# A hybrid diffusion step on one core: plain products for the feed-forward output weights, in groups of 4, 4 and 3 tile pairs

## The chip, the cores and the metric

One core of a Trainium2 chip runs the whole program in one launch. The metric is the device time of one execution in microseconds (us), the median of several. The engines named below are PE (matrix products), PEld (PE's weight loads), DVE (the vector engine), ACT (the scalar engine), POOL (GpSimd) and SP, whose queue issues the loads of the weights.

## The reference, cut to what matters

Two layers, each a mixer and then a SwiGLU feed-forward part. 512 latent and 128 context tokens go through the same weights, so a product has 640 token columns, kept as two halves of 320. The model width is 1024 (8 tiles of 128), the hidden width 2816 (22 tiles).

```python
def swiglu(h, w_in, w_out):
    gate, up = jnp.split(h @ w_in, 2, axis=-1)
    return (jax.nn.silu(gate) * up) @ w_out
...
        h = rms_norm(x, norm_ffn[l]) * (1.0 + sc2) + sh2
        x = x + g2 * swiglu(h, w_ffn_in[l], w_ffn_out[l])
```

## The kernel before, in words

Everything is float32. A float32 product is made of three products of rounded numbers: each weight tile and each activation tile is cut into a high part (`hi`, an ACT cast, L284 for weights and L450 for activations) and a low part (`lo`, what the cast left, a DVE subtraction, L285 and L451), and PE adds hi·hi, hi·lo and lo·hi. A matmul is 128x128 weights by 320 columns.

**Input side.** Hidden tile f needs its gate and its up weights, 2 x 8 tiles. For f = 0 they are taken plainly (96 matmuls). For the other 21 tiles, called blocks here (key `fs`), the two weight matrices, halved in width, and the two token halves form a 2x2 by 2x2 block product, which is done with seven products in place of eight (`quads` and `chained`): 7 x 4 x 3 = 84 matmuls where plain ones take 96. In return the weights are cut in seven pieces, four of which are sums or differences made first (`st`, L307: one by DVE, three by POOL), and the seven results are put together through three PSUM banks (ACT copies at L623, DVE adds at L579, DVE and POOL products at L625 and L621). The activations' sums (`T` tiles) are made once for a layer.

**Output side.** Hidden tiles f and f+1 make a pair. Pairs are collected in groups, given by `FFG`. Once a group is complete, all eight output tiles add this group's share to the residual X (`resid`, L539). In the first three groups (of three pairs, key `ft`) this is again done with seven products for two output tiles: 7 x 3 x 3 = 63 matmuls in place of 72. The pair's activations then need four sums or differences (POOL, L566, tiles `tt`), and seven tiles are cut into hi and lo (`hf`). The last group (two pairs, key `fo`) is plain: both activation tiles are cut whole, the weights of an output tile are cut in one piece, and `lin` (L366) runs all its matmuls (six for each hidden tile, so 24 here) into a pair of PSUM banks while the other pair is read out; the final tile goes through `prod` (L347).

**Order of the work.** Weights come in one list (`plan`) and pass through three raw buffers (`wr`, `WR`=3), of which a block or an `ft` step takes two at once. Prepared pieces go to a ring of six slots (`wp`); `feed` prepares the next piece as soon as a slot is counted free. A scheduler orders each engine's instructions when the program is built; on the chip each engine runs its own list in that order, and SP issues its loads in order, each waiting until its raw buffer has been read. After each group the first block of the next one is computed before the group's output, so that PE has work while the last pair is cut.

Of the kernel before, what the change touches and what calls it, by code (L numbers as in the profile page):

```python
# [7 lines left out]
F32 = mybir.dt.float32  # L8
F32R = mybir.dt.float32r
# [18 lines left out]
WR = 3  # L28
# [2 lines left out]
POOLED = [("even", u) for u in (18, 19, 20, 21)]  # L31
GRB = 3
WA = 2
FFG = [3, 3, 3, 2]
FPLAIN = 1
ST = 4
TT = 3
FIRST = (4, 2, 2)

ORDER = {k: ("a11", "s1", "s2", "a12", "s3", "s4", "a22") for k in ("fs", "ft")}  # L40

CONST_COLS = {}
PARAM_COLS = {}
# [169 lines left out]
class K:  # L213
    def __init__(s, nc, tc, I, O, es, dbg=None):
        s.nc, s.tc, s.I, s.O, s.es = nc, tc, I, O, es
        s.dbg = dbg or {}
        s.n = 0
        s.flip, s.sp, s.turn, s.gate = False, None, 0, None
        s.base = s.pool("base", 1)
        s.w = s.pool("w", 1)  # L220
        s.pa = s.pool("pa", 1, space=PSUM).tile([P, 512], F32, name="pa")
        s.pe = es.enter_context(ExitStack())
        s.banks(3)
        s.plan, s.parts, s.gen = [], [], None
# [70 lines left out]
    def quads(s, key, src):  # L295

        nc = s.nc
        n = src[0].shape[1] // 2
        raw = [s.t(s.w, [P, 2 * n, P], "wr", WR) for _ in range(2)]
        for r, x in zip(raw, src):  # L300
            nc.sync.dma_start(r, x)
        a11, a12, a21, a22 = (r[:, i::2, :] if key[0] == "ft" else r[:, n * i:n * i + n, :] for r in raw for i in range(2))
        whole = {"a11": a11, "a12": a12, "a22": a22}

        def made(f, x, y, op, eng):
            whole[f] = s.t(s.sp, [P, 4, P], "st", ST)[:, :n]
            eng.tensor_tensor(whole[f], x, y, op=op)  # L307
        for f in ORDER[key[0]]:
            yield 1
            if f == "s1":  # L310
                made("s1", a21, a22, ALU.add, nc.vector)
                made("s2", whole["s1"], a11, ALU.subtract, nc.gpsimd)
            elif f == "s3":
                made("s3", a11, a21, ALU.subtract, nc.gpsimd)
# [255 lines left out]
    def ffn(s, l, X, norm, ef, nxt=None):  # L570
        nc = s.nc
        n2 = lambda a: a.rearrange("p (n c) -> p n c", n=2)
        with ExitStack() as es:
# [6 lines left out]

            def val(f):
                if f not in vs:
                    vs[f] = s.t(ap, [P, T], "a", 2)
                return vs[f]

            def evac(i, n, ps):
# [3 lines left out]
                else:  # L590
                    nc.vector.tensor_tensor(a, ps, a, op=ALU.mult)

            def up(f, plain):

                i = len(slots)
                w = s.t(norm.pool if i == 2 else ap, [P, 7, 2, 320], f"hf{i}", 1, F32R)
                slots.append(w)
                b11, b12, b21, b22 = (vs[f + k][:, 320 * j:320 * j + 320] for k in range(2) for j in range(2))
                vs.pop(f), vs.pop(f + 1)
                if not plain:  # L600
                    s.sevens(lambda: s.t(late[0], [P, 320], "tt", TT), lambda x: (w[:, HF[x], 0], w[:, HF[x], 1]), b11, b12, b21, b22)
                for x, nm in ((b11, "B11"), (b12, "B12"), (b21, "B21"), (b22, "B22")):
                    if plain or nm != "B12":
                        s.split(x, w[:, HF[nm], 0], w[:, HF[nm], 1])

            def block(f):

# [16 lines left out]
                          gate0, lambda ps: add(nc.vector, p5, ps, p5), gate1,  # L624
                          lambda ps: nc.vector.tensor_tensor(a0, ps, a0, op=ALU.mult))  # L625

            def out(key, o):

                def to(*parts):
                    def read(ps):  # L630
                        for c, n in parts:
                            s.resid(X[:, o + c, :], ps, g2, o + c, n)
                    return read
                s.chained(key, lambda b, k, p: slots[k][:, HF[b], p], len(slots),
                          to((0, 0)), to((1, 1)), to((0, 1)), to((0, 0)), to((1, 1)), to((0, 1)), to((1, 0)))

            def into(f):
                if f == 0:
                    s.together([("fi", l, 0, 0), ("fi", l, 0, 1), ("fi", l, 1, 0)][:FPLAIN + 1], norm.op, KD, evac,
# [13 lines left out]
            for kind, x in ffn_order():  # L653
                if kind == "in":
                    into(x)
                elif kind == "up":
                    up(x, False)
                elif kind == "upl":
                    up(x, True)
                elif kind == "out":  # L660
                    for o in range(0, KD, 2):
                        out(("ft", l, x, o), o)
                    slots.clear()
                else:
                    s.sp = None
                    ef.close()
                    if nxt:
                        res = nxt()
                    op = lambda k, n, p: slots[k // 2][:, HF[f"B{k % 2 + 1}{n + 1}"], p]
                    s.tail([("fo", l, x, o) for o in range(KD)], op, 2 * FFG[-1], X, g2, res)  # L670
        return res


HF = {n: i % 7 for i, n in enumerate(("B11", "B21", "B22", "T1", "T2", "T3", "T4", None, None, None, "B12"))}


def ffn_order():

    r, f, done = [], 0, set()

    def into(f):
        if f not in done:
            r.append(("in", f))
            done.add(f)
    for i, n in enumerate(FFG):
        last = i == len(FFG) - 1
        f0 = f
        for _ in range(n):
            into(f)
            into(f + 1)  # L690
            r.append(("upl" if last else "up", f))
            f += 2
        if not last:
            into(f)
        r.append(("last" if last else "out", f0))
    return r
# [77 lines left out]
class NormF(Norm):  # L774
# [2 lines left out]

    def init(s, pool):
        s.F = {n: s.k.t(pool, [P, 2, 4, 320], n, 1, F32R) for n in ("B11", "B21", "B22", "T1", "T2", "T3", "T4")}
        s.pool = pool  # L780
        w = s.k.t(pool, [P, 7, 2, 320], "hf2", 1, F32R).bitcast(F32)
        s.b0 = w[:, :4].rearrange("p k i t -> p (k i) t")
        s.free = [w[:, i // 2, i % 2] for i in range(8, 14)]

# [4 lines left out]
    def put(s, n):  # L789
        if n:  # L790
            s.spread(1)
        k, nc = s.k, s.k.nc

        def full(o, b_):
            t = s.scaled(o, n)
            for i, a, b in HALF[n]:
                r = slice(a - 320 * n, b - 320 * n)
                nc.scalar.activation(b_[:, r], t[:, r], AF.Identity, bias=s.sh[:, o, i:i + 1])

        if n == 0:  # L800
# [5 lines left out]
        w = [k.t(s.ap, [P, 7, 2, 320], f"hf{i}", 1, F32R) for i in range(2)]  # L806
# [8 lines left out]
        free = s.free + [w[0][:, i // 2, i % 2].bitcast(F32) for i in range(8, 14)]  # L815
# [11 lines left out]
def plan(I):  # L827
    r = []
# [7 lines left out]
    for l in range(2):  # L836
# [4 lines left out]
        for kind, x in ffn_order():  # L841
            if kind == "in":
                w = [I[f"w_fi{l}"][x, i] for i in range(2)]
                r += [(("fs", l, x), w, None)] if x >= FPLAIN else [(("fi", l, x, i), w[i], [P, KD, P]) for i in range(2)]
            elif kind == "out":
                n = 2 * FFG[0] if x == 0 else 2 * next(g for g, e in zip(FFG, np.cumsum(FFG)) if 2 * (e - g) == x)
                r += [(("ft", l, x, o), [I[f"w_fo{l}"][o + i, :, x:x + n, :] for i in range(2)], None) for o in range(0, KD, 2)]
            elif kind == "last":
                r += [(("fo", l, x, o), I[f"w_fo{l}"][o, :, x:, :], [P, NF - x, P]) for o in range(KD)]
    return r  # L850


# [1285 lines left out]
```

## Time and profile before

| what | us |
|---|---|
| three runs, median (lowest to highest) | 1908.77 (1907.92 to 1910.2) |
| the profiled execution | 1906.5 |
| its span, first to last instruction | 1904.6 |
| feed-forward part of layer 0, first to last matmul | about 633.4 to 1091.8 |
| feed-forward part of layer 1 | about 1434 to 1898.2 |

The span is what the trace shows; the execution's own time is 1.9 us longer, and the median of the three runs is 2.3 us above the profiled execution. Times in the trace count from the start of the span.

### The profile page before, as it was taken

The page shows a single profiled execution, that of the slowest core. Times are in us where ns is not written, and L with a number is a line of the kernel's source. Part 1 is how long each engine was busy: PE and PEld are TensorE (multiplying, and loading weights), DVE is VectorE, ACT ScalarE, POOL GpSimd, SP SyncE. Part 2 cuts the span into 40 slices and gives each one's busy share as a digit, 9 for nine tenths or more (in the row PEclk, how much of TensorE's full clock was granted, in tenths as well). Part 3 has the DMA queues.
Part 4 walks back from the last instruction along what each step waited for, and adds up shares of the span by engine and source line. Part 5 has one row for each costly group of instructions (what it writes and reads, how often), then busy time and mean ns, then how long its engine had stood idle before and what let it go on. Part 6 is the DMA issues. An engine that isn't in the chain of part 4 may idle for free.

```text
span 1904.6 us, 34515 instructions
## 1 busy us (share of the span) xinstructions
PE 1748.6 (92%) x13535; PEld 1586.8 (83%) x13535; DVE 1445.2 (76%) x2651; ACT 801.3 (42%) x1654; POOL 700.5 (37%) x586
## 2 busy tenths in 40 slices
PE   6999778889999899999999999799998899999999
PEld 4887667656669789988989989788997899899899
DVE  5579998656664898998988774744749988898885
ACT  3453126423363645454553442321426544444442
POOL 2034573210110555464563103322205654645540
PEclk9998888889999999999999999899998999999999
DMA  9564443796533022222222434221321222222222
GB/s 364 166 210 158 155 148 113 189 277 186 164 100 111 23 78 73 86 74 81 79 74 82 129 109 139 85 81 43 105 74 34 67 71 86 72 84 78 73 89 94
DMA packets 101638, 214.44 MB, mean 113 GB/s; under 512 B 8317, under 2 KB 44861, under 8 KB 100069
## 3 DMA queue, kind: packets, MB, share of 16 engines
q1 hardware_dynamic: 96852, 206.14, 35.1%
q10 hardware_dynamic: 4624, 6.11, 1.1%
q8 instruction: 106, 1.74, 0.4%
q14 instruction: 56, 0.45, 0.1%
HBM read 190.68 MB, written 21.54 MB: 111 GB/s over the span
## 4 chain that ended last, share of the span: by engine, by line
PE 38%; DVE 34%; DMA 14%; issue 6%; POOL 5%; ACT 3%; SPq 0%; DVEq 0%; ACTq 0%; POOLq 0%
PE mm L366 16%; DVE wp L285 14%; DVE hf L451 5%; DMA wr<-in_w_fi 5%; PE p L347 3%; DMA wr<-in_w_fo 3%; DVE x L539 3%; PE mm L347 3%; DMA wr<-in_w_ada 3%; PE pa L495 2%; PE p L1746 2%; DVE T L451 1%; DVE a L579 1%; PE p L1769 1%; DMA D<-grd 1%
## 5 line engine op out<-in xcount | busy, mean ns | idle before, releaser
L366 PE MATMUL mm<-hi,wp 128*128 128x320 f32 x1696 | 337.9, 317 | 1.1 <-DVE x L539 0.7
L285 DVE TENSOR_TENSOR wp<-wr,wp 128x512 fp32r<-128x512 f32 (+3 forms) x282 | 287.1, 1020 | 65.5 <-ACT wp L284 62.0
L284 ACT CAST wp<-wr 128x512 fp32r<-128x512 f32 (+2 forms) x286 | 198.9, 697 | 319.9 <-PE mm L366 186.5
L366 PEld LDWEIGHTS mm<-hi,wp 128*128 128x128 f32 x1696 | 273.2, 193 | 14.5 <-issue 9.8
L285 DVE TENSOR_TENSOR wp<-st,wp 128x512 fp32r<-128x512 f32 (+1 forms) x264 | 223.9, 861 | 1.1 <-ACT wp L284 0.3
L347 PE MATMUL p<-T,wp 128*128 128x320 f32 x1260 | 207.4, 312 | 17.4 <-ACT u L623 7.8
L347 PEld LDWEIGHTS p<-T,wp 128*128 128x128 f32 x1260 | 189.6, 189 | 24.2 <-ACT u L623 9.3
L366 PE MATMUL mm<-lo,wp 128*128 128x320 f32 x848 | 200.1, 316 | 0.2 <-DVE lo L451 0.2
L284 ACT CAST wp<-st 128x512 fp32r<-128x512 f32 (+1 forms) x264 | 147.5, 579 | 111.1 <-PE p L347 45.3
L307 POOL TENSOR_TENSOR st<-st,wr 128x512 f32<-128x512 f32 (+1 forms) x66 | 93.2, 1413 | 230.4 <-DVE st L307 203.3
L347 PE MATMUL p<-B,wp 128*128 128x320 f32 x888 | 152.2, 312 | 6.3 <-DVE wp L285 5.8
L347 PE MATMUL p<-hf,wp 128*128 128x320 f32 x954 | 155.0, 310 | 3.2 <-DVE wp L285 2.2
L347 PEld LDWEIGHTS p<-hf,wp 128*128 128x128 f32 x954 | 142.8, 188 | 7.1 <-DVE wp L285 4.9
L366 PEld LDWEIGHTS mm<-lo,wp 128*128 128x128 f32 x848 | 145.6, 192 | 1.5 <-DVE lo L451 0.5
L347 PEld LDWEIGHTS p<-B,wp 128*128 128x128 f32 x888 | 134.6, 188 | 11.1 <-DVE wp L285 9.7
L347 PE MATMUL mm<-T,wp 128*128 128x320 f32 x756 | 125.5, 315 | 8.9 <-ACT u L623 2.9
L347 PEld LDWEIGHTS mm<-T,wp 128*128 128x128 f32 x756 | 114.9, 191 | 12.8 <-DVE p L579 4.7
L539 DVE SCALAR_TENSOR_TENSOR x<-mm,ada,x 128x128 f32<-128x128 f32 (+2 forms) x194 | 73.4, 419 | 61.6 <-PE mm L366 57.6
L347 PE MATMUL mm<-B,wp 128*128 128x320 f32 x624 | 106.1, 314 | 9.9 <-DVE a L625 7.5
L347 PE MATMUL mm<-hf,wp 128*128 128x320 f32 x630 | 106.8, 311 | 4.7 <-DVE x L539 2.5
L347 PEld LDWEIGHTS mm<-B,wp 128*128 128x128 f32 x624 | 96.3, 192 | 11.6 <-DVE a L625 8.3
L621 POOL TENSOR_TENSOR a<-a,p 128x320 f32<-128x320 f32 x42 | 50.5, 1203 | 149.9 <-DVE p L579 80.1
(491 smaller groups left out, 3378.7 us busy)
## 6 DMA issues: line engine op xcount, KB each, us to landing
wr<-in_w_fi SPq DMA_DIRECT2D x88, 512.0 KB, 3.5
wa<-in_w_ada SPq DMA_DIRECT2D x52, 512.0 KB, 6.5
wr<-in_w_ada SPq DMA_DIRECT2D x44, 512.0 KB, 6.5
wr<-in_w_fo SPq DMA_DIRECT2D x48, 384.0 KB, 3.1
wr<-in_w_odd SPq DMA_DIRECT2D x25, 512.0 KB, 3.6
wr<-in_w_even SPq DMA_DIRECT2D x22, 512.0 KB, 4.8
J<-scr SPq DMA_DIRECT2D x20, 512.0 KB, 7.9
scr<-vk SPq DMA_DIRECT2D x8, 640.0 KB, 3.9
```

The source lines that it names most:

```text
L284: s.nc.scalar.copy(hi, raw)
L285: (eng or s.nc.vector).tensor_tensor(lo, raw, hi.bitcast(F32), op=ALU.subtract)
L307: eng.tensor_tensor(whole[f], x, y, op=op)
L347: s.nc.tensor.matmul(out, a[:, k, :], op(k, n, p), start=(k == 0 and q == 0 and not onto), stop=(k == nk - 1 and q == 2), skip_group_check ...
L366: s.nc.tensor.matmul(ps[:, n, :320], a[:, k, :], op(k, n, p), start=(k == 0 and q == 0), stop=(k == nk - 1 and q == 2))
L451: b = (eng or s.nc.vector).tensor_tensor(lo, full, hi.bitcast(F32), op=ALU.subtract)
L495: nc.tensor.matmul(ps[32 * g:32 * g + 32, :256], s.cs[:, k, :], w[:, g * 256:(g + 1) * 256], start=(k == 0), stop=(k == KD - 1))
L539: s.nc.vector.scalar_tensor_tensor(x[:, a:b], in0=ps[:, a - 320 * n:b - 320 * n], scalar=gate[:, k, i:i + 1], in1=x[:, a:b], op0=ALU.mult, ...
L579: add = lambda eng, o, x, y: eng.tensor_tensor(o, x, y, op=ALU.add)
L621: nc.gpsimd.tensor_tensor(a1, a1, p5, op=ALU.mult)
L1746: nc.tensor.matmul(sa, qT[:, a, t, :], kf[:, a, :512], start=True, stop=True)
L1769: nc.tensor.matmul(u[64 * a:64 * a + 64, 2, :], vt[:, j, (2 * b + a) * 64:(2 * b + a) * 64 + 64], pTs[a][:, j, :], start=(j == 4), stop=(j ...
```

## The change

Three things are edited. The output weights of all groups now take the plain path, and the groups are of 4, 4 and 3 pairs; so `out`, the seven products with key `ft`, and the four sums of each pair's activations are gone, a pair's two tiles are each cut whole (128 x 2 x 320), and a third buffer `a` holds the activations. The raw weights of the blocks go through a fourth buffer, `w2`, which lives in the feed-forward part's own memory: every fourth raw load of a block takes it. The temporary tiles of the `T` sums move to the space of the fourth pair.

```diff
-FFG = [3, 3, 3, 2]
+FFG = [4, 4, 3]
...
-        raw = [s.t(s.w, [P, 2 * n, P], "wr", WR) for _ in range(2)]
-        for r, x in zip(raw, src):
-            nc.sync.dma_start(r, x)
...
+        raw = []
+        for x in src:
+
+            s.raws = (s.raws + 1) % (WR + 1)
+            raw.append(s.t(s.w, [P, 2 * n, P], "wr", WR) if s.raws else s.t(s.sp, [P, 2 * n, P], "w2", 1))
+            nc.sync.dma_start(raw[-1], x)
...
-                    vs[f] = s.t(ap, [P, T], "a", 2)
+                    vs[f] = s.t(ap, [P, T], "a", 3)
...
-                if not plain:
-                    s.sevens(lambda: s.t(late[0], [P, 320], "tt", TT), lambda x: (w[:, HF[x], 0], w[:, HF[x], 1]), b11, b12, b21, b22)
-                for x, nm in ((b11, "B11"), (b12, "B12"), (b21, "B21"), (b22, "B22")):
-                    if plain or nm != "B12":
-                        s.split(x, w[:, HF[nm], 0], w[:, HF[nm], 1])
+                for k in range(2):
+                    x = n2(vs.pop(f + k))
+                    s.split(x, w[:, 2 * k:2 * k + 2, 0], w[:, 2 * k:2 * k + 2, 1])
...
-                elif kind == "out":
-                    for o in range(0, KD, 2):
-                        out(("ft", l, x, o), o)
...
+                    nk = 2 * len(slots)
+                    hid = list(slots)
+                    op = lambda k, n, p: hid[k // 2][:, 2 * (k % 2) + n, p]
                     slots.clear()
...
+                    keys = [("fo", l, x, o) for o in range(KD)]
+                    if kind == "out":
+                        s.tail(keys, op, nk, X, g2)
```

SP's list in layer 0's second group: the loads of three blocks before (two rows for a block; `wr` is the ring of three, the number only names the tile).

```order
L301 DMA wr_8414<-in_w_fi 128x1024
L301 DMA wr_8415<-in_w_fi 128x1024
L301 DMA wr_8571<-in_w_fi 128x1024
L301 DMA wr_8572<-in_w_fi 128x1024
L301 DMA wr_8705<-in_w_fi 128x1024
L301 DMA wr_8706<-in_w_fi 128x1024
```

The same place now.

```order
L304 DMA wr_8932<-in_w_fi 128x1024
L304 DMA w_8934<-in_w_fi 128x1024
L304 DMA wr_9071<-in_w_fi 128x1024
L304 DMA wr_9073<-in_w_fi 128x1024
L304 DMA wr_9205<-in_w_fi 128x1024
L304 DMA w_9207<-in_w_fi 128x1024
```

Every fourth load goes to the fourth buffer (`w`, the tile `w2`), so that the two loads of a block and the two of the next one never share a buffer.

DVE's list for one block of layer 0's second group before (`wp` a weight cut, `st` a sum of weights, `hf` a cut of activations, `tt` a difference of activations, `a`, `p` and `u` the block's results).

```order
L307 TENSOR_TENSOR st_8604<-wr_8572 128x512
L625 TENSOR_TENSOR a_8386<-p_8390,a_8386 128x320
L285 TENSOR_TENSOR wp_8568<-wr_8415,wp_8568 128x512
L285 TENSOR_TENSOR wp_8588<-wr_8571,wp_8588 128x512
L451 TENSOR_TENSOR hf_8520<-a_8386,hf_8520 128x320
L285 TENSOR_TENSOR wp_8608<-st_8604,wp_8608 128x512
L285 TENSOR_TENSOR wp_8625<-st_8606,wp_8625 128x512
L579 TENSOR_TENSOR a_8543<-p_8549,p_8544 128x320
L451 TENSOR_TENSOR hf_8520<-tt_8529,hf_8520 128x320
L451 TENSOR_TENSOR hf_8520<-tt_8533,hf_8520 128x320
L579 TENSOR_TENSOR a_8543<-mm_8548,u_8546 128x320
L285 TENSOR_TENSOR wp_8641<-wr_8571,wp_8641 128x512
```

And for a block at the same place now.

```order
L624 TENSOR_TENSOR a_8770<-mm_8774,a_8770 128x320
L285 TENSOR_TENSOR wp_8949<-wr_8932,wp_8949 128x512
L454 TENSOR_TENSOR hf_9038<-a_8770,hf_9038 128x2x320
L285 TENSOR_TENSOR wp_8969<-st_8965,wp_8969 128x512
L582 TENSOR_TENSOR a_8904<-p_8909,u_8907 128x320
L310 TENSOR_TENSOR st_9104<-wr_9073 128x512
L285 TENSOR_TENSOR wp_8986<-st_8967,wp_8986 128x512
L582 TENSOR_TENSOR a_8904<-mm_8910,p_8905 128x320
L285 TENSOR_TENSOR wp_9002<-wr_8932,wp_9002 128x512
L582 TENSOR_TENSOR p_8906<-mm_8908,p_8906 128x320
L285 TENSOR_TENSOR wp_9022<-st_9020,wp_9022 128x512
L285 TENSOR_TENSOR wp_9052<-st_9050,wp_9052 128x512
```

The cuts of `tt` are gone, and a tile of activations is cut whole. Before, the sum `st_8604` is cut five rows behind it; now `st_9104` is made a block ahead, and none of the rows shown uses it.

ACT's list around the cast of a pair's activations before (`u` is the copy that lets PE go on in the same bank).

```order
L623 COPY p_8679<-mm_8682 128x320
L284 CAST wp_8722<-wr_8705 128x512
L450 CAST hf_8811<-a_8543 128x320
L623 COPY u_8680<-p_8681 128x320
L284 CAST wp_8742<-st_8738 128x512
L284 CAST wp_8759<-st_8740 128x512
```

And now.

```order
L622 COPY p_9045<-p_9048 128x320
L284 CAST wp_9088<-wr_9071 128x512
L453 CAST hf_9038<-a_8904 128x2x320
L622 COPY u_9046<-p_9047 128x320
L284 CAST wp_9108<-st_9104 128x512
L284 CAST wp_9125<-st_9106 128x512
```

The order is the same: the copy `u` stands behind the cast `hf`, which is now twice as wide.

## Rows read from the trace of the kernel before

**Rows 1.** The page: engines' busy time, share of the span, instructions.

```profile
PE 1748.6 (92%) x13535; PEld 1586.8 (83%) x13535; DVE 1445.2 (76%) x2651; ACT 801.3 (42%) x1654; POOL 700.5 (37%) x586
```

**Rows 2.** Timeline, PE, layer 0's mixer output: start, length, instructions.

```profile
596.29 0.75 PE L366 MATMUL mm<-hi,wp 128*128 128x320 f32 x4
...
597.17 0.75 PE L366 MATMUL mm<-hi,wp 128*128 128x320 f32 x4
```

**Rows 3.** Windows, layer 0, matmuls on prepared weights: length, busy, count, clock.

```profile
633.40:690.00 56.60, 46.63 (x266) 0.91 0.13 38
...
859.00:907.00 48.00, 44.66 (x289) 1.00 0.27 73
```

**Rows 4.** The same windows for layer 1.

```profile
1434.00:1492.00 58.00, 46.89 (x266) 0.91 0.12 37
...
1592.00:1675.00 83.00, 75.54 (x486) 0.98 0.23 72
1675.00:1715.00 40.00, 39.89 (x273) 1.00 0.30 89
```

**Rows 5.** Windows, all engines, three input stretches.

```profile
core 0: us, PE busy (x) PEld busy (x) DVE busy (x) ACT busy (x) POOL busy (x), PEclk, DMA share, GB/s
784.40:859.00 74.60, 70.30 (x470) 68.59 (x468) 67.33 (x88) 37.97 (x82) 42.22 (x30) 1.00 0.27 82
...
1027.00:1066.00 39.00, 38.26 (x259) 37.74 (x258) 33.69 (x49) 19.66 (x41) 15.52 (x11) 1.00 0.27 81
1836.00:1868.00 32.00, 31.57 (x211) 30.98 (x212) 26.04 (x37) 16.70 (x36) 12.05 (x8) 1.00 0.26 78
```

**Rows 6.** Chain that ended last, 907 to 980.5 us, share by line.

```profile
by line: DVE wp L285 30.9%; DVE hf L451 17.4%; DMA wr<-in_w_fi 14.1%; issue 7.5%; PE p L347 6.4%; PE mm L347 5.0%; DVE a L579 4.9%; POOL a L621 3.5%; POOL tt L566 2.9%; DVE a L625 2.3%; ACT wp L284 1.4%; DVE st L307 1.2%; ACT hf L450 0.6%; 
```

**Rows 7.** Waits of the weight loads, 784.4 to 906 us: total, times, longest.

```profile
PEld p L347 <- DVE wp L285: 2.3, 4, 0.8
PEld p L347 <- DVE p L579: 2.2, 2, 1.8
```

**Rows 8.** Waits of DVE, the same stretch.

```profile
DVE st L307 <- DMA wr<-in_w_fi: 7.0, 5, 2.1
```

**Rows 9.** Groups by shape, the same stretch: busy us, mean ns.

```profile
L285 DVE TENSOR_TENSOR wp<-st,wp 128x512 fp32r<-128x512 f32 x24 | 24.5, 1041 | 0.1
...
L285 DVE TENSOR_TENSOR wp<-wr,wp 128x512 fp32r<-128x512 f32 x18 | 19.8, 1104 | 0.0
...
L451 DVE TENSOR_TENSOR hf<-a,hf 128x320 fp32r<-128x320 f32 x9 | 10.6, 1177 | 1.3 <-ACT hf L450 1.3
...
L451 DVE TENSOR_TENSOR hf<-tt,hf 128x320 fp32r<-128x320 f32 x12 | 8.6, 731 | 0.4 <-ACT hf L450 0.4
...
L307 DVE TENSOR_TENSOR st<-wr 128x512 f32<-128x512 f32 x6 | 4.2, 693 | 7.1 <-DMA wr<-in_w_fi 7.0
...
L579 DVE TENSOR_TENSOR p<-p,p 128x320 f32<-128x320 f32 x4 | 1.9, 480 | 0.0
```

**Rows 10.** Groups by shape, DVE, 1066 to 1092 us, where POOL rests.

```profile
L285 DVE TENSOR_TENSOR wp<-wr,wp 128x512 fp32r<-128x512 f32 x7 | 4.8, 682 | 1.3 <-PE mm L347 1.3
```

**Rows 11.** Groups by shape, DVE, 1389 to 1417 us, layer 1's mixer output.

```profile
L285 DVE TENSOR_TENSOR wp<-wr,wp 128x1024 fp32r<-128x1024 f32 x5 | 6.0, 1215 | 0.0
...
L539 DVE SCALAR_TENSOR_TENSOR x<-mm,ada,x 128x320 f32<-128x320 f32 x4 | 2.2, 549 | 11.3 <-PE mm L366 11.3
...
L539 DVE SCALAR_TENSOR_TENSOR x<-mm,ada,x 128x192 f32<-128x192 f32 x4 | 1.6, 408 | 0.0
```

**Rows 12.** Chain that ended last, the same stretch: start, us, what.

```profile
1389.40 28.39 PE mm L366 x192
```

**Rows 13.** Timeline at 959 us: ACT's queue and the matmul behind it.

```profile
959.27 0.46 ACT L450 CAST hf<-a 128x320 fp32r<-128x320 f32 x1 [3.48 <-DVE a L625]
959.64 0.42 ACT L623 COPY u<-mm 128x320 f32<-128x320 f32 x1
...
960.11 0.41 PE L347 MATMUL mm<-T,wp 128*128 128x320 f32 x1 [1.50 <-ACT u L623]
```

More of the change, by code (lines that the diff above doesn't have):

```diff
@@ L38 @@
 FIRST = (4, 2, 2)
-ORDER = {k: ("a11", "s1", "s2", "a12", "s3", "s4", "a22") for k in ("fs", "ft")}
+ORDER = {"fs": ("a11", "s1", "s2", "a12", "s3", "s4", "a22")}
 CONST_COLS = {}
@@ L217, in __init__ @@
         s.n = 0
-        s.flip, s.sp, s.turn, s.gate = False, None, 0, None
+        s.flip, s.sp, s.turn, s.gate, s.raws = False, None, 0, None, 0
         s.base = s.pool("base", 1)
@@ L298, in quads @@
         n = src[0].shape[1] // 2
-        raw = [s.t(s.w, [P, 2 * n, P], "wr", WR) for _ in range(2)]
-        for r, x in zip(raw, src):
-            nc.sync.dma_start(r, x)
-        a11, a12, a21, a22 = (r[:, i::2, :] if key[0] == "ft" else r[:, n * i:n * i + n, :] for r in raw for i in range(2))
+        raw = []
[3 more added lines that the diff above has]
+            nc.sync.dma_start(raw[-1], x)
+        a11, a12, a21, a22 = (r[:, n * i:n * i + n, :] for r in raw for i in range(2))
         whole = {"a11": a11, "a12": a12, "a22": a22}
@@ L591, in evac, with up @@
                     nc.vector.tensor_tensor(a, ps, a, op=ALU.mult)
-            def up(f, plain):
+            def up(f):
                 i = len(slots)
-                w = s.t(norm.pool if i == 2 else ap, [P, 7, 2, 320], f"hf{i}", 1, F32R)
+                w = norm.scratch() if i == 2 else s.t(ap, [P, 4, 2, 320], f"hf{i}", 1, F32R)
                 slots.append(w)
-                b11, b12, b21, b22 = (vs[f + k][:, 320 * j:320 * j + 320] for k in range(2) for j in range(2))
-                vs.pop(f), vs.pop(f + 1)
-                if not plain:
-                    s.sevens(lambda: s.t(late[0], [P, 320], "tt", TT), lambda x: (w[:, HF[x], 0], w[:, HF[x], 1]), b11, b12, b21, b22)
-                for x, nm in ((b11, "B11"), (b12, "B12"), (b21, "B21"), (b22, "B22")):
-                    if plain or nm != "B12":
-                        s.split(x, w[:, HF[nm], 0], w[:, HF[nm], 1])
+                for k in range(2):
+                    x = n2(vs.pop(f + k))
+                    s.split(x, w[:, 2 * k:2 * k + 2, 0], w[:, 2 * k:2 * k + 2, 1])
             def block(f):
@@ L625, in block @@
                           lambda ps: nc.vector.tensor_tensor(a0, ps, a0, op=ALU.mult))
[L627 to L635, printed above, removed]
             def into(f):
@@ L656, in ffn @@
                 elif kind == "up":
-                    up(x, False)
-                elif kind == "upl":
-                    up(x, True)
-                elif kind == "out":
-                    for o in range(0, KD, 2):
-                        out(("ft", l, x, o), o)
-                    slots.clear()
[L664 to L670, printed above, removed]
+                    up(x)
+                else:
+                    nk = 2 * len(slots)
+                    hid = list(slots)
+                    op = lambda k, n, p: hid[k // 2][:, 2 * (k % 2) + n, p]
+                    slots.clear()
+                    keys = [("fo", l, x, o) for o in range(KD)]
+                    if kind == "out":
+                        s.tail(keys, op, nk, X, g2)
+                    else:
+                        s.sp = None
+                        ef.close()
+                        if nxt:
+                            res = nxt()
+                        s.tail(keys, op, nk, X, g2, res)
         return res
-HF = {n: i % 7 for i, n in enumerate(("B11", "B21", "B22", "T1", "T2", "T3", "T4", None, None, None, "B12"))}
 def ffn_order():
@@ L690, in ffn_order @@
             into(f + 1)
-            r.append(("upl" if last else "up", f))
+            r.append(("up", f))
             f += 2
@@ L779, in init @@
         s.F = {n: s.k.t(pool, [P, 2, 4, 320], n, 1, F32R) for n in ("B11", "B21", "B22", "T1", "T2", "T3", "T4")}
-        s.pool = pool
-        w = s.k.t(pool, [P, 7, 2, 320], "hf2", 1, F32R).bitcast(F32)
+        s.scratch = lambda: s.k.t(pool, [P, 7, 2, 320], "hf2", 1, F32R)
+        w = s.scratch().bitcast(F32)
         s.b0 = w[:, :4].rearrange("p k i t -> p (k i) t")
@@ L805, in put @@
             return
-        w = [k.t(s.ap, [P, 7, 2, 320], f"hf{i}", 1, F32R) for i in range(2)]
+        w = {i: k.t(s.ap, [P, 4, 2, 320], f"hf{i}", 1, F32R) for i in (0, 1, 3)}
         bs = [w[0][:, j].bitcast(F32) for j in range(4)]
@@ L814, in put @@
             k.split(b[:, 1], s.F["B22"][:, 0, j, :], s.F["B22"][:, 1, j, :])
-        free = s.free + [w[0][:, i // 2, i % 2].bitcast(F32) for i in range(8, 14)]
+        free = s.free + [w[3][:, i // 2, i % 2].bitcast(F32) for i in range(8)]
         def tmp():
@@ L844, in plan @@
                 r += [(("fs", l, x), w, None)] if x >= FPLAIN else [(("fi", l, x, i), w[i], [P, KD, P]) for i in range(2)]
[L845 to L849, printed above, removed]
+            elif kind in ("out", "last"):
+                n = 2 * next(g for g, e in zip(FFG, np.cumsum(FFG)) if 2 * (e - g) == x)
+                r += [(("fo", l, x, o), I[f"w_fo{l}"][o, :, x:x + n, :], [P, n, P]) for o in range(KD)]
     return r
```

## The prediction

> **What bounds the kernel now.** I read the page first. PE is busy 92% of the span, weight loads 83%, DVE 76% [rows 1]. That says little about one stage, because a matmul is counted for about 310 ns while the next one starts much sooner. So I took the pitch from a stretch without gaps: six matmuls start every 0.88 us (596.29 to 597.17), 146.7 ns each [rows 2]. That is the price of one matmul of 320 columns at the full clock, and everything below is counted in it.
>
> Before the change the feed-forward part of a layer has 96 + 21 x 84 + 3 x 252 + 192 = 2808 matmuls, so 411.9 us at that pitch. It lasts 458.4 us in layer 0 and 464.2 us in layer 1. PE therefore loses 46.5 + 52.3 = 98.8 us there. The windows say where:
> - The start of each part (norm, the `T` sums, the first two blocks): 56.6 us for 266 matmuls, worth 39.0, so 17.6 lost [rows 3]; in layer 1, 58.0 us for 266, so 19.0 lost [rows 4]. The granted clock there is 0.91 on average. Together 36.6 us.
> - Blocks of the middle groups: 74.6 us for 470 matmuls, 5.7 lost over 5.6 blocks, 1.0 per block [rows 5]; in layer 1, 83.0 us for 486, 11.7 lost over 5.8 blocks, 2.0 per block [rows 4].
> - Output by seven products: 48.0 us for 289, 5.6 lost [rows 3], but nothing in one of layer 1's (40.0 us for 273) [rows 4].
> - Blocks of the last group, whose pairs are cut plainly already: 39.0 us for 259 and 32.0 us for 211, 1.0 us lost in each [rows 5]. That is 2.0 us over 5.6 blocks, 0.36 per block.
>
> The last line of that list decides. What holds PE up in the middle blocks is seen in the chain: of 907 to 980.5 us, DVE's weight cuts take 30.9%, its cuts of `hf` 17.4% and the arrival of raw weights 14.1%, while PE's own lines take 11.4% [rows 6]. PE's waits there are for weight cuts and for DVE's adds on the PSUM banks [rows 7], and DVE itself waits for raw weights, 7.0 us in five waits [rows 8], since the second load of a block must wait for the buffer that the previous block still reads. DVE is busy 67.3 of 74.6 us (90%) in the middle blocks, 33.7 of 39.0 (86%) and 26.0 of 32.0 (81%) in the last ones [rows 5].
>
> **The change, part by part.**
>
> *More matmuls.* A group of n pairs takes 96n matmuls plainly, against 84n. Nine pairs in two layers: 18 x 12 = 216 more, at 146.7 ns: **+31.7 us**. These lie on PE, which is the bound of the new output stretches, so they count in full.
>
> *Output stretches.* Per output tile of a four-pair group DVE has one cut of 128x1024 at 1.215 us and three reads of the banks: 0.55 and 0.41 us and, by these, an estimated 0.34, together 2.5 us [rows 11], against 48 x 0.1467 = 7.04 us of PE. The mixer's output has exactly this form (same shapes, same line), and 192 of its matmuls take 28.39 us against 28.2 at the pitch [rows 12]. So output should lose nothing inside; I leave 0.5 us for each of the four stretches between groups, 2.0 us, and 1.3 us for the two plain ends.
>
> *Blocks.* Per pair, four cuts of differences and three of halves go and two whole cuts come. From the rows, half a pair loses 2 x 0.731 + 1.5 x 1.177 = 3.2 us of DVE and gets one cut of 640 columns [rows 9]. The trace has no such cut: it costs at most two halves, 2.35 us, and at least two undisturbed halves of about 0.48 (the add of the same width), 0.96 [rows 9]; I take 1.6. DVE's list for a block is then 4 x 1.041 + 3 x 1.104 of weight cuts, 0.69 for the sum, four adds or products of 0.48 and that cut: 11.7 us [rows 9] against 84 x 0.1467 = 12.3 us of PE. At the lower bounds (0.68 us for a weight cut while POOL rests [rows 10]) it is 8.4 us. Before it was 13.3 by the same prices (the window has 67.3 us over 5.6 blocks, 12.0 [rows 5], so these prices are a little high): as much as PE needs or more. POOL loses four differences per pair as well, and a cut beside a working POOL is 1.04 to 1.10 us against 0.68 [rows 9, 10].
>
> The last groups show what such a block loses: 0.36 us, with DMA waits still in them. 38 blocks lie outside the start stretches: 38 x 0.36 = 13.7 us. Bounds: nothing, or the old 1.0 to 2.0 per block.
>
> *Fourth raw buffer.* With four, a block's two loads never share a buffer with the previous block's. The next sum stands about a block ahead in DVE's list, so the load is there when it is reached. Removes DVE waits of 7.0 us in 121.6 [rows 8]; it is not added again, because it is part of how the loss falls to 0.36. On SP, one load into `w2` stands among the output loads; its buffer has been read by then, so nothing behind it is held. In layer 1 the first `w2` load waits for memory that the mixer output's operand held. That lies in the start stretch, and is covered there by the norm, which comes before any block.
>
> *Start.* The `T` sums stay; only the first pair's cuts get lighter. I keep 36.6 - 2 = 34.6 us, with bounds 26 (the lost clock and the weight-cut waits go) and 40.
>
> *Sum.* Lost before 98.8; after 34.6 + 13.7 + 2.0 + 1.3 = 51.6. Gain 47.2, less 31.7: **15.5 us less**. The profiled execution took 1906.5 us (span 1904.6), which becomes 1891.0; the median of the runs shown is 2.3 us above it, so **1893 us**.
>
> A rule speaks against this change. The Trainium skill (Perfetto Trace Analysis, Identifying the Most-Contended Engine) judges how near TensorE is to its limit by the busy share of weight loads and wants the most contended engine relieved first. In the middle blocks that share is 68.6 of 74.6 us, 92% [rows 5], and the change puts 216 loads more on that engine. By it the 31.7 us would be lost and little gained, which is the first rival. The rows leave 8% there, and the last groups reach 97% (37.7 of 39.0) without the seven cuts [rows 5], so I follow the rows.
>
> **The rivals.**
>
> *Slower: the blocks keep their loss.* If PE waits for the chain inside a block (bank, copy, add, next matmul) and not for DVE's load, the blocks lose what they did, and only the output stretches get smooth. Taking 5.6 us of loss for each of layer 0's three and about 0.8 in all of layer 1's, 17.6 goes to 2.0: a gain of 15.6 against 31.7, **1925 us**. It decides from 0.36 + 15.5/38 = 0.77 us of loss per block. For it: layer 1's blocks lose twice as much as layer 0's with the same instructions, so DVE's load is not all. Against it: 1.0 us in each of the two last groups.
>
> *Slower: ACT's queue.* The copy `u`, without which PE can't go on in its bank, stands behind the cast of `hf`, which waits for the block's last product on DVE. At 959.27 us that cost PE 1.50 us [rows 13], and the cast gets twice as wide. If every block paid it, 38 x 1.14 = 43 us more, **1936 us**. Against it: 24 matmuls (3.5 us) lie between the products concerned, and DVE reaches that product sooner with its load gone.
>
> *No change.* At 0.77 us per block gains and matmuls cancel: about **1909 us**.
>
> *More gain.* If four buffers and a lighter POOL take all loss from the blocks and 9 us from the start (DVE's list of 8.4 us), after is 26 + 3.3 = 29.3 us, gain 69.5 less 31.7: **1871 us**.
>
> **How the numbers follow.** My forecast (blocks lose about 0.2 to 0.6) has 0.57; more gain 0.15; no change 0.11; the blocks keep their loss 0.10; ACT's queue 0.07. Measurements of this kernel tell about 0.2% from no change, here 4 us. Faster 0.72, same 0.11, slower 0.17. The forecast's own range is 1882 to 1903. The range for 8 in 10 reaches from 1871, the end of the larger gain, to 1914, past no change and into the slower cases, leaving out their far ends.
>
> **What would show it.** In the trace after: output stretches with 48 matmuls per 7.04 us and hardly a wait of PE; DVE waiting no more for raw weights in the blocks; DVE 75 to 90% busy in blocks, about 40% in output stretches; blocks at 12.5 to 12.9 us; feed-forward parts some 7 to 9 us shorter each, the rest of the span unchanged. I am wrong if the blocks take 13.3 us or more, if PE waits for the copy `u` once in most blocks, or if the output stretches show waits for the reads of their banks.

## The result and the profile after

The changed kernel takes **1875.55 us** (median; 1873.57 to 1876.41), the kernel before 1908.35 us (1904.55 to 1910.2) in the same comparison: a ratio of 0.983, 95% interval 0.9815 to 0.9846. It is faster by 1.7%. The forecast of 1893 us had the direction right and 17 us too little gain: 15.5 us were forecast and 32.8 came. The rival "more gain" (1871 us) lies much nearer. The profiled execution has a span of 1873.6 us, 31.0 us shorter than before.

The page after: first the engines' busy time, share of the span and instructions (the same line of before is [rows 1]), then the chain that ended last, by engine.

```profile
PE 1750.8 (93%) x13751; PEld 1611.7 (86%) x13751; DVE 1231.2 (66%) x2225; ACT 735.3 (39%) x1420; POOL 512.1 (27%) x442
...
PE 74%; DVE 15%; DMA 5%; issue 2%; ACT 2%; POOL 1%; SPq 0%; ACTq 0%; DVEq 0%; POOLq 0%
```

And the chain of the kernel before, from its page:

```profile
PE 38%; DVE 34%; DMA 14%; issue 6%; POOL 5%; ACT 3%; SPq 0%; DVEq 0%; ACTq 0%; POOLq 0%
```

216 matmuls are added, as the count 13751 against 13535 says, and 214 us of DVE's work are gone. DVE and DMA, 48% of the chain before, are 20% of it now, and PE itself has gone from 38% to 74%.

The next fence holds windows over both feed-forward parts, for matmuls on prepared weights: stretch, length, PE's busy time (and matmuls), granted clock, DMA share, GB/s. They answer to [rows 3] and [rows 4]. The rows of layer 0 are the start, an output, blocks, an output and the last output; those of layer 1 the start, blocks and the last output.

```profile
634.00:690.00 56.00, 46.89 (x268) 0.88 0.14 40
...
760.00:813.00 53.00, 53.00 (x364) 1.00 0.26 79
813.00:915.00 102.00, 102.00 (x697) 1.00 0.28 87
915.00:967.70 52.70, 52.70 (x362) 1.00 0.24 75
...
1035.00:1080.00 45.00, 44.13 (x298) 1.00 0.39 133
...
1423.20:1481.00 57.80, 46.66 (x275) 0.94 0.15 45
...
1757.80:1825.30 67.50, 67.50 (x462) 1.00 0.24 72
1825.30:1870.00 44.70, 44.02 (x297) 1.00 0.25 90
```

From the end of the start stretch to the last output, PE is busy without a gap, in blocks and outputs alike: 53.0 us hold 364 matmuls, 102.0 us hold 697, which at 146.7 ns [rows 2] are 53.4 and 102.2 us (a matmul that lies across an edge counts whole). The weight loads have no wait from 690 to 1030 and from 1481 to 1825 us, where before they had several in 120 us [rows 7].

Now the two parts whole, for matmuls on prepared weights: before, then after.

```profile
633.40:1098.80 465.40, 433.13 (x2808) 0.99 0.26 78
1434.00:1901.50 467.50, 433.15 (x2808) 0.99 0.24 75
```

```profile
634.00:1080.00 446.00, 436.02 (x2916) 0.98 0.26 82
1423.20:1870.00 446.80, 434.97 (x2916) 0.99 0.25 78
```

The ends given ahead of the prediction for the kernel before, 1091.8 and 1898.2 us, lie too early: 2763 and 2789 of each part's 2808 matmuls stand in those windows. The parts lasted 465.4 and 467.5 us, not 458.4 and 464.2, and together they are 40.1 us shorter now. The span is only 31.0 us shorter, and most of the difference lies between the layers. PE there before, from the last products of layer 0 to the first product of layer 1, and the sums of squares that the next norm needs (`nacc`):

```profile
1096.78 1.93 PE L347 MATMUL mm<-hf,wp 128*128 128x320 f32 x12
1098.54 0.72 PE L735 MATMUL pa<-consts,nacc 128*128 128x1 f32 x6
...
1104.19 0.63 PE L396 MATMUL p<-hi,wp 128*128 128x320 f32 x1 [1.31 <-ACT hi L768]
```

```profile
L729 DVE TENSOR_TENSOR nacc<-nacc,nsq x13: 481/483/492, 1079.4 to 1099.2; 128x320 f32<-128x320 f32 x13
```

The same after:

```profile
1076.84 2.81 PE L350 MATMUL p<-hf,wp 128*128 128x320 f32 x18
1086.55 1.44 PE L722 MATMUL pa<-consts,nacc 128*128 128x1 f32 x6 [6.90 <-DVE nacc L716]
...
1093.39 0.64 PE L399 MATMUL p<-hi,wp 128*128 128x320 f32 x1 [1.24 <-ACT hi L755]
```

```profile
L716 DVE TENSOR_TENSOR nacc<-nacc,nsq x14: 481/491/493, 1080.3 to 1087.0; 128x320 f32<-128x320 f32 x14
```

Before, DVE made these sums between its reads of the last outputs. Now all 14 stand behind the last read, and PE waits 6.90 us for them: from the last product of layer 0 to the first of layer 1 it takes 13.7 us in place of 5.5.

Two stretches with all engines, most of an output of four pairs and nearly eight blocks behind it (columns as in [rows 5]; the row of 813 to 915 us above begins with that output's last 7 us):

```profile
760.00:806.00 46.00, 46.00 (x316) 46.00 (x315) 16.96 (x27) 7.16 (x8) 5.66 (x4) 1.00 0.30 91
820.00:915.00 95.00, 95.00 (x650) 95.00 (x649) 74.55 (x98) 52.70 (x100) 36.16 (x27) 1.00 0.28 87
```

DVE is busy 78% of the blocks' time (90% before) and 37% of the output's; POOL 38% of the blocks' (57% before, 42.22 of 74.6 us).

The chain of 915 to 1035 us, first by line, then one piece (start, us, what), against [rows 6]:

```profile
by line: PE mm L369 41.6%; PE p L350 36.7%; PE mm L350 21.9%
...
921.95 45.76 PE mm L369 x312
```

Where DVE's cuts had 48% of the chain and raw weights 14%, there is nothing but PE: 312 matmuls of an output in 45.76 us, 146.7 ns each. And DVE's groups by shape in 813 to 915 us (busy us, mean ns, idle before), against [rows 9]:

```profile
L285 DVE TENSOR_TENSOR wp<-st,wp 128x512 fp32r<-128x512 f32 x31 | 28.3, 925 | 6.4 <-ACT wp L284 6.0
...
L454 DVE TENSOR_TENSOR hf<-a,hf 128x640 fp32r<-128x640 f32 x8 | 6.6, 822 | 1.4 <-ACT hf L453 1.4
...
L310 DVE TENSOR_TENSOR st<-wr 128x512 f32<-128x512 f32 x3 | 2.1, 686 | 0.2 <-DMA wr<-in_w_fi 0.2
```

### The profile page after: what moved, and what is told of

It is laid out like the page before. It is cut to its first block, busy times and chain, and to the rows that moved or that the text cites. A ratio compares the mean times of both kernels' runs of the same rounds, so it can differ in the third digit from the quotient of the medians.

```text
span 1873.6 us, 33809 instructions
## 1 busy us (share of the span) xinstructions
PE 1750.8 (93%) x13751; PEld 1611.7 (86%) x13751; DVE 1231.2 (66%) x2225; ACT 735.3 (39%) x1420; POOL 512.1 (27%) x442
## 4 chain that ended last, share of the span: by engine, by line
PE 74%; DVE 15%; DMA 5%; issue 2%; ACT 2%; POOL 1%; SPq 0%; ACTq 0%; DVEq 0%; POOLq 0%
PE mm L369 28%; PE p L350 18%; PE mm L350 12%; PE pa L498 2%; DMA wr<-in_w_ada 2%; DVE tmp L1383 1%; PE p L1731 1%; DVE X L1384 1%; DVE wp L285 1%; PE p L1754 1%; PE p L1994 1%; DVE T L454 1%; PE p L1741 1%; DVE W L1906 1%; DVE nsq L743 1%
## 5 line engine op out<-in xcount | busy, mean ns | idle before, releaser
L284 ACT CAST wp<-wr 128x1024 fp32r<-128x1024 f32 (+2 forms) x225 | 186.7, 831 | 510.8 <-PE mm L369 363.4
L285 DVE TENSOR_TENSOR wp<-wr,wp 128x512 fp32r<-128x512 f32 (+2 forms) x221 | 255.9, 1160 | 82.6 <-ACT wp L284 75.3
L369 PE MATMUL mm<-hf,wp 128*128 128x320 f32 x1812 | 269.5, 309 | 1.0 <-DVE a L624 0.7
L369 PEld LDWEIGHTS mm<-hf,wp 128*128 128x128 f32 x1812 | 266.6, 188 | 2.0 <-DVE a L624 1.2
L350 PE MATMUL p<-T,wp 128*128 128x320 f32 x1224 | 197.7, 311 | 0.1
L285 DVE TENSOR_TENSOR wp<-st,wp 128x512 fp32r<-128x512 f32 x168 | 149.2, 904 | 23.7 <-ACT wp L284 21.7
L310 POOL TENSOR_TENSOR st<-st,wr 128x512 f32<-128x512 f32 x42 | 57.1, 1360 | 326.9 <-DVE st L310 114.2
L284 ACT CAST wp<-st 128x512 fp32r<-128x512 f32 x168 | 101.7, 621 | 101.8 <-PE p L350 46.2
L350 PE MATMUL mm<-B,wp 128*128 128x320 f32 x600 | 98.8, 309 | 0.8 <-DVE wp L285 0.8
L620 POOL TENSOR_TENSOR a<-a,p 128x320 f32<-128x320 f32 x42 | 40.8, 971 | 145.7 <-DVE p L582 135.7
L310 POOL TENSOR_TENSOR st<-wr,st 128x512 f32<-128x512 f32 x42 | 72.4, 1724 | 9.0 <-DVE wp L285 8.3
```

Source lines behind the costliest of these rows:

```text
L284: s.nc.scalar.copy(hi, raw)
L285: (eng or s.nc.vector).tensor_tensor(lo, raw, hi.bitcast(F32), op=ALU.subtract)
L350: s.nc.tensor.matmul(out, a[:, k, :], op(k, n, p), start=(k == 0 and q == 0 and not onto), stop=(k == nk - 1 and q == 2), skip_group_check ...
L369: s.nc.tensor.matmul(ps[:, n, :320], a[:, k, :], op(k, n, p), start=(k == 0 and q == 0), stop=(k == nk - 1 and q == 2))
L620: nc.gpsimd.tensor_tensor(a1, a1, p5, op=ALU.mult)
```

## The experiments

Two things were changed at once: the outputs became plain, which also drops the pairs' sums (`tt`) from POOL's and DVE's lists, and the blocks got a fourth raw buffer. My theory was that DVE's load in the blocks decides ("load"); the rival, that the arrival of raw weights does ("buffer"). The groups changed with the outputs, from 3, 3, 3 and 2 pairs to 4, 4 and 3, which a run of its own tests.

**The buffer alone (e_seven4).** The kernel before, with the fourth raw buffer; to make room, the `tt` tiles have two buffers.

```diff
-TT = 3
+TT = 2
...
-        raw = [s.t(s.w, [P, 2 * n, P], "wr", WR) for _ in range(2)]
...
+            s.raws = (s.raws + 1) % (WR + 1)
+            raw.append(s.t(s.w, [P, 2 * n, P], "wr", WR) if s.raws else s.t(s.sp, [P, 2 * n, P], "w2", 1))
```

> The kernel before with the fourth raw buffer alone: output by seven products in groups of 3, 3, 3 and 2, four sums of activations per pair as before (and two temporary tiles for them in place of three, to make room). Theory 'load' (the cuts of the activation sums filled DVE's list, raw weights were a symptom): DVE still needs about 12.0 us of a block's 12.3, so the waits for raw weights go but PE's losses stay: 1895 to 1910 us. Rival 'buffer' (the second raw load came too late, and that alone held the chain): blocks run without loss and there are 216 matmuls fewer than in the change, 31.7 us: 1840 to 1858 us.

Measured: 1868.97 us (1863.05 to 1870.76), ratio 0.9788 (0.9768 to 0.9808). Neither theory had it: more than load allowed, less than buffer promised, and faster than the change. Of this kernel, windows of an output and the blocks behind it in layer 0, and an output in layer 1 (columns as in [rows 3]), then the waits of the weight loads from 690 to 1030 us:

```profile
732.00:775.00 43.00, 40.49 (x265) 0.97 0.27 83
775.00:850.00 75.00, 73.23 (x496) 1.00 0.25 80
1523.00:1565.00 42.00, 42.00 (x289) 1.00 0.32 98
```

```profile
PEld mm L349 <- issue: 7.6, 3, 2.7
PEld mm L349 <- DVE p L581: 5.1, 3, 2.0
```

Counted at 146.7 ns a matmul, its blocks lose about 0.4 us each (2.2 over 5.9) with DVE busy 94% of that window (70.45 of 75.00 us). The output shown of layer 0 still loses 4.1 us, that of layer 1 nothing.

**Control (e_tt2).** The kernel before with `TT = 2` alone.

> The kernel before with two temporary tiles for the sums in place of three, a control for e_seven4. Both theories: within 5 us of the kernel before, 1904 to 1914 us.

Measured: 1906.3 us, one run, inside the spread of before. The buffer made the difference, not the smaller ring.

**The sums alone (e_buf3).** The change with three raw buffers.

```diff
-            raw.append(s.t(s.w, [P, 2 * n, P], "wr", WR) if s.raws else s.t(s.sp, [P, 2 * n, P], "w2", 1))
+            raw.append(s.t(s.w, [P, 2 * n, P], "wr", WR))
```

> The changed kernel with three raw buffers, all else as in the change (plain output, groups of 4, 4 and 3). Theory 'load': DVE needs about 9.4 us of a block and waits some 1.3 us for raw weights, still under 12.3: 1875 to 1882 us, PE's losses outside the start below 5 us. Rival 'buffer': blocks lose 1 to 2 us again as before, 40 blocks: 1905 to 1940 us.

Measured: 1876.84 us (1875.1 to 1878.41), ratio 0.9834 (0.9818 to 0.9851): 1.3 us from the change. DVE still waits for raw weights in this kernel; its waits from 690 to 1030 us (total, times, longest):

```profile
DVE st L310 <- DMA wr<-in_w_fi: 21.4, 15, 3.8
```

But the weight loads have no wait there. DVE's waits cost nothing here, since its list is short enough to catch up before PE needs the next piece. In the change, the fourth buffer is therefore worth next to nothing.

**The sums put back (e_sums4).** The change, with each pair's four differences made and cut, into a tile that nobody reads; it does so for all eleven pairs of a layer, the kernel before for nine.

```diff
+                b11, b12, b21, b22 = (vs[f + k][:, 320 * j:320 * j + 320] for k in range(2) for j in range(2))
+                d = s.t(late[0], [P, 2, 320], "dum", 1, F32R)
+                s.sevens(lambda: s.t(late[0], [P, 320], "tt", 2), lambda x: (d[:, 0], d[:, 1]), b11, b12, b21, b22)
```

> The changed kernel with the four sums of activations of each pair made and cut again, into a tile that nobody reads (POOL 4 x 1.15 us, ACT 4 x 0.46, DVE 4 x 0.5 to 0.9 per pair); plain output, four raw buffers. Theory 'load': DVE at 11 to 12 us of 12.3 per block, losses of 0.5 to 1 us per block come back: 1890 to 1915 us. Rival 'buffer': within 3 us of the change, 1873 to 1879 us.

Measured: 1896.24 us (1895.84 to 1901.08), ratio 0.9942 (0.9926 to 0.9959). The sums cost 20.7 us where four buffers are there, so buffer fell. The blocks of this kernel from 820 to 920 us and from 690 to 760 us, all engines:

```profile
820.00:920.00 100.00, 97.54 (x658) 96.13 (x657) 85.80 (x110) 54.44 (x110) 56.66 (x41) 1.00 0.26 80
690.00:760.00 70.00, 66.39 (x442) 64.55 (x441) 64.97 (x81) 38.69 (x81) 43.50 (x32) 1.00 0.26 83
```

DVE is back at 86%, POOL at 57%. At 146.7 ns a matmul PE loses 3.5 us in the first row, over nearly eight blocks, and 5.2 in the second, over a little more than five. DVE's list is not all of it. The longest wait of the weight loads from 690 to 1030 us is for ACT's copy `u`, and just before one such wait ends ACT does this:

```profile
PEld p L350 <- ACT u L625: 3.0, 3, 1.2
```

```profile
898.34 0.46 ACT L453 CAST dum<-tt 128x320 fp32r<-128x320 f32 x1 [0.60 <-POOL tt L569]
898.70 0.42 ACT L625 COPY u<-p 128x320 f32<-128x320 f32 x1
```

The copy stands behind the cast of a sum that waits for POOL. Of the 9.3 us that the weight loads wait from 690 to 1030 us, 5.0 are for ACT and 4.3 for DVE. The unread copies also share one tile, so that DVE waits 15.3 us for ACT there and ACT 5.5 for DVE, while the kernel before has a place for each. So the 20.7 us are what the sums cost on three engines; no run takes them from DVE alone.

**The sums put back, three buffers (e_sums3).** Both edits together: against before, it is mainly the kind of the outputs and their groups that differ.

> e_sums4 with three raw buffers: plain output, the unread activation sums, the late raw weights. It completes the square of sums (with, without) and raw buffers (three, four) on the change's code. Theory 'either relief is enough' (DVE's work and its waits for raw weights add up in one list, and PE loses only what their sum exceeds its own 12.3 us per block): the buffer, worth 1.3 us without the sums, is worth far more with them: 1912 to 1930 us. Rival 'additive' (sums cost 20.7 us, the buffer 1.3 us, each by itself): 1896 to 1900 us.

Measured: 1907.8 us (1902.83 to 1910.05), ratio 1.0004 (0.9991 to 1.0016): no change. It fell between the two expectations. The waits of the weight loads, 690 to 1030 us:

```profile
PEld p L350 <- DVE p L582: 4.8, 6, 1.5
PEld mm L350 <- DVE p L582: 3.0, 4, 1.8
```

DVE's add on a bank is late, as before [rows 7]. The medians stand thus:

| outputs, sums | three buffers | four buffers |
|---|---|---|
| plain, without sums | 1876.84 | 1875.55 (the change) |
| plain, sums made | 1907.8 | 1896.24 |
| by seven products, sums made | 1908.35 (before) | 1868.97 |

Either relief helps, and they do not add: with the sums in DVE's list the fourth buffer is worth 11.6 us, without them 1.3; the sums cost 31.0 us with three buffers and 20.7 with four. Plain outputs in groups of 4, 4 and 3 are worth 0.6 us with three buffers (their 31.7 us of matmuls against what the outputs by seven products lost), and cost 27.3 us with four, where those outputs lose less. Both differences hold the groups too: the four plain kernels of the table take 13.7 us between the layers, before and e_seven4 5.5 and 5.9. By subtraction, which no run tests, plain outputs alone would be worth about 9 us with three buffers and cost about 19 with four.

**Group sizes (e_3332).** The change with the groups of before.

```diff
-FFG = [4, 4, 3]
+FFG = [3, 3, 3, 2]
```

> The changed kernel with groups of 3, 3, 3 and 2 pairs, all else as in the change: the same 2916 matmuls per layer, one stretch of output more, the residual read and written once more. Theory 'size of the groups plays no part': 1873 to 1879 us. Rival 'fewer groups were part of the gain' (each change from blocks to output costs PE 1 to 2 us): 1880 us or more.

Measured: 1871.81 us (1866.17 to 1875.56), ratio 0.9825 (0.9806 to 0.9843), faster than either expectation, and no wait of the weight loads from 690 to 1030 us. The times alone don't part it from the change (1873.57 to 1876.41), but the traces do. PE between the layers in e_3332:

```profile
1074.92 1.93 PE L350 MATMUL mm<-hf,wp 128*128 128x320 f32 x12
...
1082.21 0.64 PE L399 MATMUL p<-hi,wp 128*128 128x320 f32 x1 [1.32 <-ACT hi L755]
```

From the last product of layer 0 to the first of layer 1 it takes 5.4 us, where the change takes 13.7; the two feed-forward parts, from first to last product, take 2.4 us longer together (893.3 against 890.9). So the sizes count: a last group of three pairs costs some 8 us there, and the change some 6 in all by the traces (the medians are 3.7 apart). Between the layers it goes the same way in every run: the change, e_buf3, e_sums3, e_sums4 and e_mixed, whose layer 0 ends with three pairs, take 13.7 us there, and before, e_tt2, e_3332, e_seven4 and e_seven4p, with two, take 5.4 to 6.5. Why DVE's list then has the next norm's sums behind the last output stays open.

The stretch ahead of the first feed-forward part takes 628.7 to 635.5 us over the profiled executions of these ten kernels. Totals that differ by a few us are therefore better compared part by part.

**The buffers' turn (e_seven4p).** e_seven4 with the same buffer first in both layers, to see whether the turn of the buffers makes layer 0's outputs lose and layer 1's not.

```diff
+            s.raws = 2
```

> e_seven4 with the turn of the raw buffers set so that layer 0 takes them in the order in which layer 1 takes them. In e_seven4 the output by seven products loses 3 to 4 us per group in layer 0 and nothing in layer 1. If the turn is what makes the difference (a step's second load in the lone buffer against one of the three): layer 0's output loses nothing either, 1856 to 1862 us. If it is something else of layer 0: 1865 to 1872 us.

Measured: 1869.53 us (1867.11 to 1871.78), ratio 0.9806 (0.979 to 0.9821), with nearly the same waits in layer 0 as e_seven4. The turn is not the cause.

**The better half of each (e_mixed).** Layer 0 as in the change, layer 1 by seven products, both with four buffers. The cut edit is against the kernel before, and the buffers' part of it is left out here.

```diff
-FFG = [3, 3, 3, 2]
+FFG = {0: [4, 4, 3], 1: [3, 3, 3, 2]}
...
+                elif kind == "out" and l == 0:
+                    hid = list(slots)
+                    slots.clear()
...
                 elif kind == "out":
                     for o in range(0, KD, 2):
```

> Four raw buffers in both layers; layer 0 gives its output weights as plain products over groups of 4, 4 and 3 as in the change, layer 1 by seven products over groups of 3, 3, 3 and 2 as in the kernel before. The theory that the two layers stand by themselves, each held only by its own VectorE list: layer 0 as in the change (446 us) and layer 1 as in the kernel with seven products and four buffers, whose outputs in layer 1 lost nothing: 1858 to 1866 us, and in layer 1's output stretches TensorE busy for the whole stretch. The rival, that what seven products lose goes with the kind of output and lands in whichever layer uses it: 1868 to 1875 us, and 3 to 4 us lost in each output group of layer 1.

Measured: 1879.64 us (1879.29 to 1880.43), ratio 0.9848 (0.9832 to 0.9864), a higher median than either parent, and above both expectations. Layer 1's part in e_mixed, then in e_seven4, columns as in [rows 3], and the waits of the weight loads in e_mixed from 1470 to 1840 us:

```profile
1423.50:1874.40 450.90, 427.11 (x2808) 0.98 0.25 77
```

```profile
1418.00:1857.90 439.90, 423.00 (x2808) 0.98 0.25 79
```

```profile
PEld mm L349 <- issue: 6.5, 3, 2.4
PEld mm L349 <- DVE p L582: 4.7, 3, 2.0
```

The two kinds of wait that e_seven4 had in layer 0 are now in layer 1, three times each, so they don't belong to a layer; the rival was right in this. Layer 1's part is 11.0 us longer than in e_seven4, layer 0's 9.0 us shorter, and between the layers e_mixed takes 13.7 us against 5.9, since its layer 0 ends with three pairs. These add up to 9.8 us; the medians are 10.7 apart. What the waits call "issue" can be followed at one of them. The timeline of PE's weight loads, and of DVE, at 1563 us (start, us, what):

```profile
1563.13 0.34 PEld L349 LDWEIGHTS p<-hf,wp 128*128 128x128 f32 x2
1565.55 3.61 PEld L349 LDWEIGHTS mm<-hf,wp 128*128 128x128 f32 x18 [2.08 <-issue]
```

```profile
1561.99 0.69 DVE L309 TENSOR_TENSOR st<-w 128x512 f32<-128x512 f32 x1 [1.00 <-DMA w<-in_w_fi]
...
1563.66 1.31 DVE L285 TENSOR_TENSOR wp<-wr,wp 128x384 fp32r<-128x384 f32 x1
1564.89 0.54 DVE L541 SCALAR_TENSOR_TENSOR x<-mm,ada,x 128x320 f32<-128x320 f32 x1
```

The load starts at 1565.55, 0.12 us after DVE's read of an `mm` bank (1564.89 + 0.54) has ended; PE's own row there has the read (`x`, L541) as what ended 1.85 us of waiting. The read stood behind a sum that waited 1.00 us for raw weights and a cut of 1.31 us. In a seven-product output, several products add onto a bank that DVE must read first, with one other product between (nine matmuls for a group of three, 1.3 us), so a read late by more than that holds PE. Which order of DVE's list brings the waits about in one layer and not in the other stays open.

The fastest version tried is **e_seven4**, 2.1% under before and faster than the change; e_3332's range reaches into its own.

## Why the prediction was right and wrong

- **More matmuls, +31.7 us: right in count and price.** 216 more, and outputs run at 146.7 ns (45.76 us for 312).
- **Output stretches: no loss inside, right.** I left 0.5 us for each of the four transitions and 1.3 us for the ends; the transitions show nothing, and the last outputs have 0.9 and 0.7 us in their windows.
- **Start, 34.6 us: right.** The two start windows hold 268 and 275 matmuls in 56.0 and 57.8 us, so 16.7 + 17.5 = 34.2 us are lost.
- **Lost before, 98.8 us: 10.3 us too little.** The windows behind this term end 45 and 19 matmuls before the parts do, but all 2808 were taken off. With the parts' whole 465.4 + 467.5 us it is 109.1.
- **"The rest of the span unchanged": it grew by 9.1 us**, 8.3 of them between the layers, where PE now waits for the next norm's sums. The forecast had this at nothing. e_3332 shows that the last group of three pairs brings it.
- **Blocks, 38 x 0.36 = 13.7 us: this step failed.** The feed-forward parts last 446.0 + 446.8 = 892.8 us and hold 5832 matmuls, worth 855.6, so 37.2 us are lost where I forecast 51.6. 34.2 of them lie in the starts and 1.6 in the last outputs, which leaves 1.4 us for all 38 blocks and the transitions, forecast at 13.7 + 2.0. In the blocks from 820 to 915 us there is no loss at all: 650 matmuls are worth 95.3 us and take 95.0. That relieving the lists clears the blocks was the forecast mechanism (e_sums4 shows that it isn't DVE's list alone); the size of what is left was wrong.

Of the 31.0 us that the span became shorter, 15.5 were forecast. The blocks, transitions and starts account for about 14.4 more, the loss before that was counted too small for 10.3 more, and the growth elsewhere for 9.1 less. The last two nearly cancel by luck: the blocks look like the whole error and are one error of three.

The 0.36 came from the last groups of before, where 2.0 us were missing over 5.6 blocks, and I took that as what a block without the seven cuts loses. The waits of the weight loads in those two stretches of before, 1027 to 1066 and 1836 to 1868 us, say what it was:

```profile
PEld mm L347 <- DVE x L539: 0.8, 1, 0.8
PEld p L347 <- DVE wp L285: 0.4, 1, 0.4
...
PEld p L347 <- DVE wp L285: 0.7, 2, 0.5
```

In each stretch 0.8 us was one wait at its edge (at 1028.5 and 1836.2 us), for DVE's read of a bank (`x`) of the seven-product output just before it. That output is gone in the change. What belonged to the blocks was 0.4 and 0.7 us of weight cuts. The stretch was a sample of the wrong thing: a border effect divided by blocks.

- **DVE's list of 11.7 us for a block: 2 us too long.** The window has 74.55 us for 650 matmuls, 7.7 blocks, so 9.6 us against 12.3 us of PE. The whole cut of 128x640 takes 0.822 us, below my lower bound of 0.96, not the 1.6 I took, and the cuts of `st` 0.925 in place of 1.041 beside a POOL that works less. The list is then a fifth shorter than PE's time for the block, not a twentieth, and the 0.36 should have looked too high. That points to the rival with 8.4 us, which came true for the blocks but not for the start.
- **Fourth buffer: it does what I said, but it isn't what counts.** DVE's wait for raw weights in the middle blocks fell from 7.0 us in 121.6 to 0.2 in 102. e_buf3 shows that, with the sums gone, 21.4 us of such waits are harmless. With the sums there it is worth 11.6 us, and with the seven-product outputs 39.4: the forecast gave the buffer no price of its own.
- **"The blocks keep their loss" fell**: with the sums gone they lose nothing, so the chain inside a block wasn't the bound. **"ACT's queue" fell** too: no wait for the copy `u` in the blocks after, though the cast ahead of it is twice as wide. But it was part of the loss before: the weight loads waited 12.8 us for `u` from 690 to 1066 and 1492 to 1868 us, of 65.8 us in all. With the sums back it returns (4.1 us in five waits in e_sums4's 690 to 1030 us).
- **The rule that I set aside.** The Trainium skill (Perfetto Trace Analysis, Identifying the Most-Contended Engine) judges by the busy share of weight loads, beside the share of peak arithmetic rate, how near TensorE is to its limit, and wants the most contended engine optimized first. The trace agrees with the share as a measure of what is left: at 92%, 8% remained, and 5.7 of 74.6 us were lost. That 216 more loads would then only cost, as the prediction drew from it, did not come: what was lost there was PE waiting for the other engines, and the share of the blocks after is 95.00 of 95.00 us.

## What to carry to other kernels

An in-order engine's work and its waits for data add up against the bound engine's time for the same step: in this kernel, with one of them relieved far enough the other cost nothing, so test each part alone before paying 31.7 us of matmuls for both. A loss per step taken from a short stretch is to be split into its waits first, because one wait at its border can be most of it. Check that the windows of a part hold all of its matmuls, and look at what comes behind the part: here a gain of 40 us in the parts lost 8 between them. Gains of two halves needn't add; the mixture has to be run.

## What the runs showed of the hardware

- A DVE cut took longer while POOL worked. The two rows of cuts of 128x320 before (800 to 870 us: shortest, median and longest, ns) and the row of 128x640 after (813 to 915 us):

```profile
L451 DVE TENSOR_TENSOR hf<-tt,hf x11: 474/491/1589, 804.8 to 867.4; 128x320 fp32r<-128x320 f32 x11
L451 DVE TENSOR_TENSOR hf<-a,hf x8: 486/1155/1584, 803.5 to 864.4; 128x320 fp32r<-128x320 f32 x8
```

```profile
L454 DVE TENSOR_TENSOR hf<-a,hf x8: 811/824/826, 818.0 to 912.6; 128x640 fp32r<-128x640 f32 x8
```

- Of all 115 such cuts of halves in before (690 to 1030 and 1492 to 1830 us), the 40 with no POOL instruction beside them took 0.48 us on average, the 53 beside POOL nearly all the time 1.36 us. So the whole cut of 0.82 us costs 1.7 undisturbed halves; it came out under one disturbed half because it ran with POOL at rest (35 of 36 whole cuts in the same windows after).
- The cuts of `st` of 128x512 in the same windows took 0.68 us with POOL at rest beside them (30 of 126) and 1.01 us on average before; after, 0.69 us (81 of 144) and 0.91 us on average. Taking work from POOL shortened DVE's list as well.
- PE waited for nothing while DVE waited 21.4 us in 340 for DMA (e_buf3): the six slots of prepared weights were enough there.
